# Four projection buffers and two small ones in PSUM, other banks for two kinds of transposes, and a priority for the weights' steps

## The chip, the cores and the metric

The kernel runs on one core of a Trainium2 chip. The metric is the device time of one execution in microseconds. The kernel before takes 2092.26 us, the median of three runs (2090.07 to 2092.64).

The engines are TensorE (PE, matmuls and transposes), VectorE (DVE), ScalarE (ACT), GpSimd (POOL) and SyncE (SP, which issues the DMAs). Each runs its own instructions in order and waits for the others by semaphores. PE writes into PSUM, a memory of eight banks of 128 partitions x 2 KiB; 128x512 values in float32 fill one bank.

## The reference, cut to what matters

One decoder block with two branches from one normalized input, for 2048 tokens and width 1024:

```python
h = rmsnorm(x, norm_g)
glu_in, conv_gate, q, k, v, attn_gate, merge_logits = split(h @ w_in)   # 2048, 1024, 1024, 256, 256, 1024, 2048 columns

a, b = split(glu_in)                       # convolution branch
c = a * sigmoid(b)
c = depthwise_causal_conv(c, 31 taps) + bias
c = silu(layernorm(c))
y_conv = (c * silu(conv_gate)) @ w_conv_out

q, k = rope(q), rope(k)                    # attention branch: 16 query heads, 4 key/value heads of 64
p = softmax(q k^T / 8 over the last 128 keys, with one sink per head)
y_attn = ((p v) * silu(attn_gate)) @ w_attn_out

g_conv, g_attn = split(sigmoid(merge_logits))
x = x + (g_conv * y_conv + g_attn * y_attn) @ w_out
out = rmsnorm(x, final_norm_g)
```

All values are float32. The result has the shape (1, 2048, 1024).

## The kernel before, in words

The tokens are worked in two sweeps of 1024. In each, columns of `w_in` are taken in pieces of 128: h, transposed, lies in SBUF as `hT`, and a piece gives 128 columns of the projection for 1024 tokens, in two halves of 512. To keep float32's accuracy, each number is split in a high and a low part (`whi`, `wlo`; both have type fp32r), and a product is three matmuls: high by high, high by low, low by high. A half is 8 slices of the inner dimension by 3 = 24 matmuls of 128x512 into one PSUM buffer `mm_...` (line 281), and is then read (evacuated) by ACT or DVE.

`load_w` (line 244 on) brings one piece of weights in two halves of the inner dimension: a DMA of the raw values on SP's queue, the cast of the high part on ACT (line 253), and in the first sweep the low part as a difference on POOL (line 242), which is stored in DRAM (`d_lo`, line 263) and only loaded in the second sweep. Buffers for `raw`, `whi` and `wlo` are four each.

PSUM is cut in three pools: `mm` for projections (3 buffers of a bank), `tp` for transposes and value products (3 buffers of a bank), `sc` for attention scores (1 buffer of two banks).

PE's order is written by hand: a generator yields the pieces one after another, and between their matmuls a planner (`Line`) puts the steps of other chains at due times reckoned in a model of PE's pace: the transposes of x (`tpf`, lines 360 and 361), the value transposes (`tpv`, lines 497 and 499), and for each of 32 blocks of attention per sweep the scores (`sc`), the transposes of the probabilities (`tpp`) and the products with the values (`ov`). Instructions on the other engines are ordered by a scheduler: it follows the program's order, and steps inside `tc.high_priority(offset=PRIO)` with PRIO = 60 are taken as if they stood that much earlier. Evacuations and the steps of the chains have it; `load_w` has not, which is called through `prefetch` in `project` one piece ahead.

The values of a sweep are two pieces (`v_item`, i = 0 and 1), each in two halves of 512 tokens. For each of these four, ACT copies the projected half to SBUF (`vs`), PE transposes it in four steps into a `tp` buffer (`tpv`), and ACT and DVE read that buffer: `vf` is ACT's copy of it, `vd` DVE's difference of neighbouring blocks (lines 502 and 503), and `vt` its two parts, high by ACT (line 513) and low by DVE (line 242). Four buffers are asked of a pool of three, whose first is free by the fourth.

The convolution is 31 steps per piece on DVE (`cv`, line 393, 128x1024), 248 per sweep, which the planner lays between other steps. Rope takes the projections of q and k in pairs `a` and `b` (lines 460 to 467, four DVE reads of a pair's buffers per half), joins them on POOL (lines 468 and 469) and splits the result on ACT and DVE. Gates (`ag`, `cg`, `ma`, `mc`) and the sigmoid of the GLU are evacuated by ACT (lines 434 and 415).

Of the kernel before, what the change touches and what calls it, by code (L numbers as in the profile page):

```python
# [12 lines left out]
F32 = mybir.dt.float32  # L13
# [6 lines left out]
P = 128  # L20
# [28 lines left out]
PRIO = 60  # L49
# [4 lines left out]
def hybrid_block(ctx: ExitStack, tc: tile.TileContext, x, par_d, w_in, w_conv, sinks, w_attn, w_out,  # L54
# [5 lines left out]
    slots = ctx.enter_context(tc.tile_pool(name="slots", bufs=1))  # L60
    stage = ctx.enter_context(tc.tile_pool(name="stage", bufs=4))
    work = ctx.enter_context(tc.tile_pool(name="work", bufs=2))
    mm_ps = ctx.enter_context(tc.tile_pool(name="mm_ps", bufs=3, space=bass.MemoryType.PSUM))
    tp_ps = ctx.enter_context(tc.tile_pool(name="tp_ps", bufs=3, space=bass.MemoryType.PSUM))
    sc_ps = ctx.enter_context(tc.tile_pool(name="sc_ps", bufs=1, space=bass.MemoryType.PSUM))
    dram = ctx.enter_context(tc.tile_pool(name="dram", bufs=1, space=bass.MemoryType.DRAM))

# [3 lines left out]
    def f(ap):  # L71
        return ap.bitcast(F32)
# [8 lines left out]
    def slot(tag, shape, dt, name):  # L81
        n = int(np.prod(shape[1:]))
        full = HALO + T + 2 if tag in WIDE else 1024
        t = slots.tile([P, full], dt, tag=tag, name=name)
        v = t[:, 0:n]
        if len(shape) == 3:
            v = v.rearrange("p (a b) -> p a b", b=shape[2])
        elif len(shape) == 4:
            v = v.rearrange("p (a b c) -> p a b c", b=shape[2], c=shape[3])
        return v  # L90

    def t2k(name, dt=F32):
        return work.tile([P, TH], dt, tag="t2k", name=name, bufs=5)
# [140 lines left out]
    line = Line()  # L234
# [6 lines left out]
    def split_lo(out_, full, hi, eng):  # L241
        eng.tensor_tensor(out=out_, in0=full, in1=f(hi), op=ALU.subtract)  # L242

    def load_w(src, name):

        parts = []
        at = lo_at.setdefault((src.tensor.name, src.offset), len(lo_at))
        for kh in range(2):
            raw = stage.tile([P, 4, P], F32, tag="raw", name=f"raw_{name}{kh}")
            nc.sync.dma_start(out=raw, in_=src[:, 4 * kh:4 * kh + 4, :])  # L250
            hi = stage.tile([P, 4, P], F32R, tag="whi", name=f"whi_{name}{kh}")
            lo = stage.tile([P, 4, P], F32R, tag="wlo", name=f"wlo_{name}{kh}")
            act.copy(hi, raw)  # L253
            if (at, kh) in lo_stored:
                nc.sync.dma_start(out=f(lo), in_=d_lo[at, kh])
            else:
                split_lo(lo, raw, hi, pool)
            parts.append((hi, lo))

        def keep(kh):  # L260
            if (at, kh) not in lo_stored:
                lo_stored.add((at, kh))
                nc.sync.dma_start(out=d_lo[at, kh], in_=f(parts[kh][1]))

        return lambda k: (parts[k // 4][0][:, k % 4, :], parts[k // 4][1][:, k % 4, :]), keep

    def project(src, rhs, name, evac, halves=(0, 1)):

        got = {}

        def prefetch():
            got["w"] = load_w(src, name)

        def blocks():
            for half in halves:
                ps = mm_ps.tile([P, TH], F32, tag="mm", name=f"mm_{name}{half}")
                for k in range(KC):
                    whi, wlo = got["w"][0](k)
                    r = rhs(k, half)
                    for i, (a, b) in enumerate(((whi, r[:, 0, :]), (whi, r[:, 1, :]), (wlo, r[:, 0, :]))):  # L280
                        pe.matmul(out=ps, lhsT=a, rhs=b, start=(k == 0 and i == 0),  # L281
                                  stop=(k == KC - 1 and i == 2))
                    if k == KC - 1:
                        with tc.high_priority(offset=PRIO):
                            evac(half, ps)
                    if half == halves[-1] and k % 4 == 3:
                        got["w"][1](k // 4)
                    yield 3 * MM_US

        def by_halves():  # L290
            return [project(src, rhs, f"{name}{h}", evac, (h,)) for h in range(2)]

        return prefetch, blocks, by_halves
# [5 lines left out]
    def make_tiles(tags, half, name):  # L299
        return [slot(tags[half * 8 + k], [P, 2, TH], F32R, f"{name}{half}_{k}") for k in range(KC)]  # L300
# [43 lines left out]
    def build_h_first(half, xs):  # L344

        ss = work.tile([P, 2, 4], F32, tag="ss0", name=f"ssf{half}")
        for j in range(4):
            xt = xs[j]
            sq = slot(C[j], [P, D], F32, f"sqf{half}_{j}")
            act.activation(out=sq, in_=xt, func=AF.Square, accum_out=ss[:, 0, j:j + 1])  # L350
            act.activation(out=ss[:, 1, j:j + 1], in_=ss[:, 0, j:j + 1], func=AF.Sqrt, bias=eps,
                           scale=1.0 / D)
            dve.reciprocal(out=ss[:, 0, j:j + 1], in_=ss[:, 1, j:j + 1])
            dve.tensor_scalar(out=xt, in0=xt, scalar1=ss[:, 0, j:j + 1], scalar2=None, op0=ALU.mult)
        yield 0.0, 6.0
        if half == 1:
            ht[1] = make_tiles(h_tags[0], 1, "hT0_")
        for k in range(KC):
            tp = tp_ps.tile([P, 4, P], F32, tag="tp", name=f"tpf{half}_{k}")
            for j in range(4):  # L360
                pe.transpose(out=tp[:, j, :], in_=xs[j][:, k * P:(k + 1) * P], identity=ident)
            d = ht[half][k].rearrange("p a (j t) -> p a j t", t=P)
            act.activation(out=d[:, 0], in_=tp, func=AF.Copy, scale=g_norm[:, k, :])
            dve.scalar_tensor_tensor(out=d[:, 1], in0=tp, scalar=g_norm[:, k, :], in1=f(d[:, 0]),
                                     op0=ALU.mult, op1=ALU.subtract)
            yield 0.44, 0.8

    def program():
        for s in range(NSWEEP):
            yield from sweep(s)  # L370

    def sweep(s):
# [116 lines left out]
            return store  # L489


        vt, vd = {}, {}

        def v_item(i):
            def chain(half, vs):
                yield 0.0, 7.0
                tp = tp_ps.tile([P, 4, P], F32, tag="tp", name=f"tpv{s}_{i}_{half}")
                for j in range(4):
                    pe.transpose(out=tp[:, j, :], in_=vs[:, j * P:(j + 1) * P], identity=ident)
                vf, d = (t2k(f"{n}{s}_{i}_{half}").rearrange("p (b c) -> p b c", c=P) for n in ("vf", "vd"))  # L500
                act.copy(vf, tp)
                dve.tensor_tensor(out=d[:, 1:4], in0=tp[:, 1:4], in1=vf[:, 0:3], op=ALU.subtract)
                dve.tensor_tensor(out=d[:, 0], in0=tp[:, 0], in1=v_last[:, i], op=ALU.subtract)
                act.copy(v_last[:, i], vf[:, 3])
                for j in range(2):
                    bp = 2 * half + j
                    if i == 0:
                        vt[bp] = slot(AT[bp], [P, 2, NKV, 2 * HD], F32R, f"vt{s}_{bp}")
                        vd[bp] = slot((X + AT[15:])[bp], [P, 2, NKV, 2 * HD], F32R, f"vd{s}_{bp}")
                    for full, to in ((tp, vt), (d, vd)):  # L510
                        part = full[:, 2 * j:2 * j + 2, :].rearrange("p b (g d) -> p b g d", d=HD)
                        hi, lo = (to[bp][:, :, 2 * i:2 * i + 2, a * HD:(a + 1) * HD] for a in range(2))
                        act.copy(hi, part)
                        split_lo(lo, part, hi, dve)
                yield 0.44, 0.0

            def ev(half, ps):
                vs = t2k(f"vs{s}_{i}_{half}")
                act.copy(vs, ps)
                line.start(chain(half, vs))  # L520

            return project(w_in[C_V // P + i], h_rhs, f"v{i}{s}", ev)
# [238 lines left out]
        if s == 0:  # L761
            halves = [item[2]() for item in glu_items(0) + others[:1]]
            halves[0][0][0]()
            xs = load_first(1)
            for _ in build_h_first(0, x_first):
                pass
            line.start(build_h_first(1, xs))
            for half in range(2):
                for i, item in enumerate(halves):
                    yield ((lambda: None) if half == i == 0 else item[half][0],) + item[half][1:]  # L770
            glu_after.pop(0)
# [185 lines left out]
```

## Time and profile before

| | before |
|---|---|
| median of 3 runs | 2092.26 us (2090.07 to 2092.64) |
| profiled execution | 2090.34 us |
| its span, first to last instruction | 2088.4 us |
| PE busy (matmuls) | 2044.0 us, 98% |
| DVE busy | 1391.3 us, 67% |
| ACT busy | 1032.4 us, 49% |
| POOL busy | 483.2 us, 23% |
| mean granted clock of PE | 0.995 |

The profile is that of one execution, whose own time is 1.9 us below the median. "Busy" is the time in which an engine worked on an instruction; a wait is put down to the instruction of another engine that ended last before it. In a row of the timeline stand the start in us, the duration, the engine, the line in the kernel, the operation, output and inputs, shapes, and in brackets the idle time before it and what ended it.

### The profile page before, as it was taken

What the parts mean: (1) busy time and instruction counts of PE and PEld (TensorE: products, weight loads), DVE (VectorE), ACT (ScalarE), POOL (GpSimd) and SP (SyncE); (2) the same over time, 40 slices, a digit from 0 to 9 for tenths busy, and PEclk for the clock granted to TensorE, in tenths of its full rate; (3) what the DMA queues carried; (4) which work ended last, traced back from release to release, by engine and by line L of the source; (5) the groups of instructions that cost most, each with busy time, mean ns of one, the idle gap of its engine ahead of it and who ended that gap; (6) DMA issues with size and microseconds to landing.
All of it is one profiled execution on the core that took longest, in us unless ns stands there. A gap on an engine that the chain in (4) does not pass through costs nothing.

```text
span 2088.4 us, 27452 instructions
## 1 busy us (share of the span) xinstructions
PE 2044.0 (98%) x9256; PEld 1671.7 (80%) x9256; DVE 1391.3 (67%) x1901; ACT 1032.4 (49%) x2265; POOL 483.2 (23%) x336
## 2 busy tenths in 40 slices
PE   7999999998999999999999999999999999999998
PEld 6787888886777888888888888888888888888887
DVE  4979779998988348123559596698888934341324
ACT  6221377666667646112442214766777774621222
POOL 2445433433334222243001131121111110000200
PEclk9999999999999999999999999999999999999999
DMA  7344555554455775646344456555555578574432
GB/s 250 133 144 157 178 166 157 158 163 146 148 152 182 254 238 184 202 142 221 101 151 132 141 161 204 172 158 175 175 163 164 175 225 259 162 236 146 140 119 81
DMA packets 265820, 355.90 MB, mean 170 GB/s; under 512 B 28112, under 2 KB 126544, under 8 KB 265680
## 3 DMA queue, kind: packets, MB, share of 16 engines
q1 hardware_dynamic: 265680, 354.16, 53.3%
q8 instruction: 73, 1.20, 0.2%
q14 instruction: 67, 0.55, 0.1%
HBM read 234.51 MB, written 119.54 MB: 170 GB/s over the span
## 4 chain that ended last, share of the span: by engine, by line
PE 70%; DVE 4%; issue 2%; ACT 1%; DMA 0%; POOL 0%; SPq 0%; DVEq 0%; POOLq 0%; ACTq 0%
PE o L877 9%; PE mm_mc L281 8%; PE mm_yc L281 8%; PE mm_ya L281 8%; PE mm_ma L281 7%; PE mm_ga L281 5%; PE mm_cg L281 5%; PE mm_ag L281 4%; PE mm_gb L281 4%; DVE cv L393 2%; PE mm_q_a L281 2%; PE mm_q_b L281 2%; PE ov L614 2%; PE sc L566 2%; PE mm_v L281 1%
## 5 line engine op out<-in xcount | busy, mean ns | idle before, releaser
L393 DVE SCALAR_TENSOR_TENSOR cv<-glu,par,cv 128x1024 f32<-128x1024 f32 x480 | 675.9, 1408 | 6.7
L605 POOL TENSOR_SCALAR_AFFINE_SELECT pc<-pt 128x1024 fp32r<-128x1024 f32 x60 | 102.7, 1711 | 452.9 <-DVE pt L242 419.6
L877 PE MATMUL o<-wo,mT 128*128 128x512 f32 x768 | 181.3, 394 | 0.0
L877 PEld LDWEIGHTS o<-wo,mT 128*128 128x128 f32 x768 | 143.1, 188 | 32.1
L281 PE MATMUL mm_cg<-hT,whi_cg 128*128 128x512 f32 x512 | 163.2, 400 | 4.6 <-ACT glu L415 3.0
L281 PE MATMUL mm_ma<-hT,whi_ma 128*128 128x512 f32 x512 | 162.9, 399 | 4.0 <-ACT whi_ma L253 4.0
L281 PE MATMUL mm_ga<-hT,whi_ga 128*128 128x512 f32 x512 | 161.0, 395 | 0.2 <-ACT whi_ga L253 0.2
L281 PE MATMUL mm_ag<-hT,whi_ag 128*128 128x512 f32 x512 | 160.9, 395 | 0.0
L281 PE MATMUL mm_gb<-hT,whi_gb 128*128 128x512 f32 x512 | 160.6, 395 | 0.0
L281 PE MATMUL mm_mc<-hT,whi_mc 128*128 128x512 f32 x512 | 159.6, 393 | 0.0
L281 PE MATMUL mm_yc<-uT,whi_yc 128*128 128x512 f32 x512 | 159.4, 392 | 0.0
L281 PE MATMUL mm_ya<-aT,whi_ya 128*128 128x512 f32 x512 | 158.7, 391 | 0.0
L281 PEld LDWEIGHTS mm_cg<-hT,whi_cg 128*128 128x128 f32 x512 | 95.3, 191 | 25.2 <-ACT glu L415 3.4
L281 PEld LDWEIGHTS mm_ma<-hT,whi_ma 128*128 128x128 f32 x512 | 95.1, 190 | 23.9 <-ACT whi_ma L253 4.4
L281 PEld LDWEIGHTS mm_yc<-uT,whi_yc 128*128 128x128 f32 x512 | 96.2, 188 | 21.9
L281 PEld LDWEIGHTS mm_mc<-hT,whi_mc 128*128 128x128 f32 x512 | 96.0, 188 | 21.8
L281 PEld LDWEIGHTS mm_ya<-aT,whi_ya 128*128 128x128 f32 x512 | 96.1, 188 | 20.9
L281 PEld LDWEIGHTS mm_ga<-hT,whi_ga 128*128 128x128 f32 x512 | 94.5, 188 | 20.8 <-ACT whi_ga L253 1.0
L281 PEld LDWEIGHTS mm_gb<-hT,whi_gb 128*128 128x128 f32 x512 | 94.7, 188 | 20.0
L281 PEld LDWEIGHTS mm_ag<-hT,whi_ag 128*128 128x128 f32 x512 | 94.2, 188 | 19.7 <-ACT whi_ag L253 0.3
L584 ACT ACTIVATE ss<-ss,st 128x128 f32<-128x128 f32 x256 | 99.9, 391 | 19.2 <-DVE st L579 18.6
L815 POOL TENSOR_TENSOR lmc<-lmc,mp 128x512 f32<-128x512 f32 x32 | 41.9, 1309 | 275.5 <-DVE lmc L814 267.1
(363 smaller groups left out, 4356.4 us busy)
## 6 DMA issues: line engine op xcount, KB each, us to landing
qk<-d_q SPq DMA_DIRECT2D x256, 64.0 KB, 2.7
d_a<-ss SPq DMA_DIRECT2D x128, 128.0 KB, 1.9
aT<-d_a SPq DMA_DIRECT2D x32, 512.0 KB, 6.1
qk<-d_k SPq DMA_DIRECT2D x240, 64.0 KB, 2.1
raw_gb<-in_w_in_dram SPq DMA_DIRECT2D x34, 256.0 KB, 4.0
raw_ga<-in_w_in_dram SPq DMA_DIRECT2D x34, 256.0 KB, 3.4
raw_ag<-in_w_in_dram SPq DMA_DIRECT2D x32, 256.0 KB, 3.8
d_ag<-ag SPq DMA_DIRECT2D x32, 256.0 KB, 2.1
```

Of the source, the lines that this page charges most:

```text
L281: pe.matmul(out=ps, lhsT=a, rhs=b, start=(k == 0 and i == 0), stop=(k == KC - 1 and i == 2))
L393: dve.scalar_tensor_tensor(out=cv[c], in0=glu[c][:, j:j + T], scalar=tap(c, j), in1=cv[c], op0=ALU.mult, op1=ALU.add)
L566: pe.matmul(out=o, lhsT=q[:, h, :], rhs=r, start=(j == 0), stop=(j == 1))
L584: act.activation(out=sb[:, h, :], in_=sb[:, h, :], func=AF.Exp, scale=SCALE, bias=ngm[:, h:h + 1], accum_out=den[:, h:h + 1])
L605: pool.affine_select(out=pc, in_=f(pt), pattern=[[0, 2], [0, GQ], [1, P]], compare_op=ALU.is_ge, fill=0.0, base=0, channel_multiplier=-1)
L614: pe.matmul(out=ov, lhsT=vv, rhs=pp[:, i % 2], start=(i == 0), stop=(i == nm - 1))
L815: pool.tensor_tensor(out=g, in0=g, in1=mp[e][:, half * TH:(half + 1) * TH], op=ALU.add)
L877: pe.matmul(out=ps, lhsT=a[:, c0:c0 + P], rhs=r, start=(k == 0 and i == 0), stop=(k == KC - 1 and i == 2))
```

## The change

Four edits:

- The pool of projection buffers has 4 banks and the pool of small buffers 2.
- The first transposes of x (`tpf0`, half 0) take their buffers from the projection pool, those of half 1 from the small pool as before.
- The value transposes of the two halves of a piece share one tile of two banks in the pool of the scores, each half in a bank of its own; before, each had a tile of the small pool.
- The loads of the weights and their casts and splits are emitted with a priority: offset PRIO when the planner's time is past 30, else the same wrapper with offset 0.

```diff
-    mm_ps = ctx.enter_context(tc.tile_pool(name="mm_ps", bufs=3, space=bass.MemoryType.PSUM))
-    tp_ps = ctx.enter_context(tc.tile_pool(name="tp_ps", bufs=3, space=bass.MemoryType.PSUM))
+    mm_ps = ctx.enter_context(tc.tile_pool(name="mm_ps", bufs=4, space=bass.MemoryType.PSUM))
+    tp_ps = ctx.enter_context(tc.tile_pool(name="tp_ps", bufs=2, space=bass.MemoryType.PSUM))
     sc_ps = ctx.enter_context(tc.tile_pool(name="sc_ps", bufs=1, space=bass.MemoryType.PSUM))
@@ project
         def prefetch():
-            got["w"] = load_w(src, name)
+            with tc.high_priority(offset=PRIO if line.t > 30.0 else 0):
+                got["w"] = load_w(src, name)
@@ build_h_first
         for k in range(KC):
-            tp = tp_ps.tile([P, 4, P], F32, tag="tp", name=f"tpf{half}_{k}")
+            pool_, tag = ((mm_ps, "mm"), (tp_ps, "tp"))[half]
+            tp = pool_.tile([P, 4, P], F32, tag=tag, name=f"tpf{half}_{k}")
@@ v_item
-        vt, vd = {}, {}
+        vt, vd, tpv = {}, {}, {}
 
         def v_item(i):
             def chain(half, vs):
                 yield 0.0, 7.0
-                tp = tp_ps.tile([P, 4, P], F32, tag="tp", name=f"tpv{s}_{i}_{half}")
+                if half == 0:
+                    tpv[i] = sc_ps.tile([P, 2, 4, P], F32, tag="sc", name=f"tpv{s}_{i}")
+                tp = tpv[i][:, half]
                 for j in range(4):
                     pe.transpose(out=tp[:, j, :], in_=vs[:, j * P:(j + 1) * P], identity=ident)
```

PE's instructions stand in the same order in both kernels. What they wait for differs. On PE, the place of the second and third group of value transposes in the first sweep (`tpv` with `vs_0_1` and `vs_1_0`; `mm_v` is the projection of v, `mm_q_a` the first of q), before:

```order
L281 MATMUL mm_v_792<-hT_1_0_313,wlo_v_660 128x512
L499 MATMUL tpv_0_1_796<-ident_r,vs_0_1_725 128x128 [waits Activation_49]
L281 MATMUL mm_v_792<-hT_1_1_314,whi_v_659 128x512 x2
...
L281 MATMUL mm_q_a_858<-hT_0_0_124,wlo_q_a_731 128x512 [waits Pool_49]
L499 MATMUL tpv_1_0_862<-ident_r,vs_1_0_790 128x128 [waits Activation_49]
L281 MATMUL mm_q_a_858<-hT_0_1_125,whi_q_a_730 128x512 x2
```

and in the changed kernel:

```order
L282 MATMUL mm_v_792<-hT_1_0_313,wlo_v_660 128x512
L503 MATMUL tpv_0_748<-ident_r,vs_0_1_725 128x128 [waits DVE_49]
L282 MATMUL mm_v_792<-hT_1_1_314,whi_v_659 128x512 x2
...
L282 MATMUL mm_q_a_857<-hT_0_0_124,wlo_q_a_731 128x512 [waits Pool_49]
L503 MATMUL tpv_1_861<-ident_r,vs_1_0_790 128x128 [waits DVE_49]
L282 MATMUL mm_q_a_857<-hT_0_1_125,whi_q_a_730 128x512 x2
```

The second group writes the tile of the first (`tpv_0_748`), and both wait for a count of DVE's semaphore where they waited for one of ACT's.

On ACT, at the start (`hT_0` are the scaled transposes of x's first half, `sqf` the squares of its second half, `whi_gb_000` and `whi_gb_001` the two halves of the first weight), before:

```order
L253 CAST whi_gb_000_139<-raw_gb_000_137 128x512
L253 CAST whi_gb_001_145<-raw_gb_001_143 128x512
L363 ACTIVATE hT_0_4_128<-tpf_4_206,par 128x512
L363 ACTIVATE hT_0_5_129<-tpf_5_213,par 128x512
L350 ACTIVATE sqf_0_235,ssf_234<-xf_0_149 128x1024
L363 ACTIVATE hT_0_6_130<-tpf_6_220,par 128x512
```

and in the changed kernel:

```order
L253 CAST whi_gb_000_139<-raw_gb_000_137 128x512
L365 ACTIVATE hT_0_4_128<-tpf_4_206,par 128x512
...
L351 ACTIVATE sqf_1_240,ssf_234<-xf_1_151 128x1024
L365 ACTIVATE hT_0_7_131<-tpf_7_227,par 128x512
L352 ACTIVATE ssf_234<-ssf_234,eps_t 128x1
L351 ACTIVATE sqf_2_245,ssf_234<-xf_2_153 128x1024
L253 CAST whi_gb_001_145<-raw_gb_001_143 128x512
```

The cast of the second half now stands behind three of the four squares; on SP's queue its load stands behind the first three loads of that half of x, where it stood ahead of them.

On ACT, near the end of the first sweep's attention (block 2_7's exponentials and scaled copies `ss`, block 2_6's cast `pt`, the weight `ma_01`), before:

```order
L584 ACTIVATE ss_2_7_5081,st_2_7_5084<-ss_2_7_5081,st_2_7_5084 128x128
L599 CAST pt_2_6_5161<-tpp_2_6_5155 128x512
L589 ACTIVATE ss_2_7_5081<-ss_2_7_5081,st_2_7_5084 128x128 x4
L253 CAST whi_ma_01_5133<-raw_ma_01_5131 128x512
L617 COPY ss_2_5_4801<-ov_2_5_5184 64x256 x2
```

and in the changed kernel:

```order
L588 ACTIVATE ss_2_7_5079,st_2_7_5082<-ss_2_7_5079,st_2_7_5082 128x128
L253 CAST whi_ma_01_5131<-raw_ma_01_5129 128x512
L593 ACTIVATE ss_2_7_5079<-ss_2_7_5079,st_2_7_5082 128x128 x4
L603 CAST pt_2_6_5159<-tpp_2_6_5153 128x512
L621 COPY ss_2_5_4799<-ov_2_5_5182 64x256 x2
```

The weight's cast has moved ahead of the four scaled copies and of the cast of `pt`. Seven second weight halves in the first sweep have moved in this manner.

## The prediction

> **What bounds the kernel now.** I read the page first: which engine is full, and whether the share of the others says anything.
>
> ```profile
> span 2088.4 us, 27452 instructions
> ...
> PE 2044.0 (98%) x9256; PEld 1671.7 (80%) x9256; DVE 1391.3 (67%) x1901; ACT 1032.4 (49%) x2265; POOL 483.2 (23%) x336
> ```
>
> TensorE (PE) is short of the span by 44 us. All that buffers and priorities can win lies in those 44 us and in matmuls that run at a lower clock; all that they can lose is new idle time on PE. So next, PE's busy time by stretches (columns: stretch, its length, busy time and count on each engine, granted clock, DMA share, GB/s):
>
> ```profile
> 310.00:360.00 50.00, 48.68 (x231) 39.79 (x231) 48.42 (x64) 34.21 (x76) 19.09 (x13) 1.00 0.52 158
> ...
> 460.00:510.00 50.00, 45.92 (x215) 36.48 (x214) 49.35 (x60) 36.57 (x78) 14.60 (x9) 1.00 0.49 151
> 510.00:560.00 50.00, 45.08 (x198) 36.44 (x198) 43.20 (x58) 30.40 (x76) 19.39 (x13) 0.93 0.46 141
> 560.00:610.00 50.00, 46.74 (x218) 37.51 (x217) 41.59 (x56) 36.37 (x87) 19.35 (x13) 1.00 0.52 153
> 610.00:660.00 50.00, 45.90 (x206) 37.08 (x205) 49.49 (x62) 33.51 (x75) 15.78 (x10) 0.93 0.52 163
> 660.00:1130.00 470.00, 470.00 (x2098) 384.39 (x2097) 225.97 (x375) 192.68 (x422) 110.94 (x83) 1.00 0.56 184
> ...
> 1160.00:1500.00 340.00, 340.00 (x1571) 280.26 (x1570) 269.44 (x349) 181.17 (x415) 60.50 (x38) 1.00 0.57 172
> ```
>
> From 660 us on PE is never idle. The second sweep (from about 1100) has nothing to win, and whatever PE loses there, or still has to its debit at 660, arrives at the end in full. Before 660 the attention stage (235 to 660) holds 17.7 us of idle PE in five of these stretches (1.32 + 4.08 + 4.92 + 3.26 + 4.10), and VectorE (DVE) is the fullest of the others there. What PE waits for, over the whole span (total, times, longest):
>
> ```profile
> PE mm_ma L281 <- ACT whi_ma L253: 4.0, 1, 4.0
> PE mm_q_b L281 <- DVE rb_q__1_1524 L467: 3.4, 1, 3.4
> PE mm_cg L281 <- ACT glu L415: 3.0, 1, 3.0
> ...
> PE tpv L499 <- ACT vs L519: 2.1, 1, 2.1
> ...
> PE mm_q_b L281 <- DVE ra_q__0_1408 L461: 1.3, 1, 1.3
> ...
> PE tpf L361 <- DVE hT L364: 0.5, 1, 0.5
> ```
>
> The `mm_q_b` waits and the `mm_cg` wait are for a projection buffer to be emptied; `mm_ma` waits for a weight's cast. These are what the fourth buffer and the priority reach. But DVE and ScalarE (ACT) have waits of their own between 235 and 700 us:
>
> ```profile
> DVE pt L242 <- ACT pt L599: 24.5, 8, 3.8
> ...
> DVE glu L419 <- PE mm_ga L281: 4.9, 1, 4.9
> ```
> ```profile
> ACT ss L621 <- DVE ss L619: 50.4, 28, 3.3
> ```
>
> Their big waits are for each other; the one on PE is at the stage's start, 4.9 us. So in that stage softmax, value products and convolution run as a chain on DVE and ACT with a pace of its own, and PE's idle time is mostly PE keeping step with it.
>
> **The value transposes.** This is the largest term. Rows of PE, DVE and ACT around the first sweep's, then PE and DVE in the second:
>
> ```profile
> 85.63 0.60 PE L499 MATMUL tpv<-ident_r,vs 128*128 128x128 f32 x4
> ...
> 93.93 0.66 PE L499 MATMUL tpv<-ident_r,vs 128*128 128x128 f32 x4 [2.11 <-ACT vs L519]
> ```
> ```profile
> 79.36 12.35 DVE L393 SCALAR_TENSOR_TENSOR cv<-glu,par,cv 128x1024 f32<-128x1024 f32 x8
> ...
> 95.68 0.42 DVE L242 TENSOR_TENSOR vt<-tpv,vt 128x256 fp32r<-128x256 f32 x1
> 96.02 0.55 DVE L502 TENSOR_TENSOR vd<-tpv,vf 128x384 f32<-128x384 f32 x1
> ...
> 98.88 0.41 DVE L242 TENSOR_TENSOR vt<-tpv,vt 128x256 fp32r<-128x256 f32 x1
> ...
> 106.21 0.41 DVE L242 TENSOR_TENSOR vt<-tpv,vt 128x256 fp32r<-128x256 f32 x1
> ```
> ```profile
> 94.20 0.59 ACT L501 COPY vf<-tpv 128x512 f32<-128x512 f32 x1
> ```
> ```profile
> 1135.84 0.60 PE L499 MATMUL tpv<-ident_r,vs 128*128 128x128 f32 x4
> ...
> 1141.81 0.60 PE L499 MATMUL tpv<-ident_r,vs 128*128 128x128 f32 x4
> ```
> ```profile
> 1139.50 0.42 DVE L242 TENSOR_TENSOR vt<-tpv,vt 128x256 fp32r<-128x256 f32 x1
> ```
>
> The row at 85.63 is the second of four groups (item 0, half 1); it has a buffer of its own and waits for ACT alone. In the changed order it writes the second bank of the tile whose first bank is item 0's half 0, and its wait is one on DVE; so is that of the third group, which takes the tile anew. I read the second's wait as that for DVE's last read of half 0. DVE is late with it: eight convolution steps of 12.35 us stand ahead of the reads, and the last ends at 95.68 + 0.42 = 96.10. PE is in order: its q projection stands behind the transposes. Loss 96.10 - 85.63 = 10.5 us.
>
> Such a gap also costs clock. After the 3.43 us gap of the wait on `rb_q` the trace has
>
> ```profile
> 198.65 1.03 PE L281 MATMUL mm_q_b<-hT,whi_q_b 128*128 128x512 f32 x2 [3.43 <-DVE rb_q__1_1524 L467]
> ...
> 202.37 0.63 PE L281 MATMUL mm_q_b<-hT,whi_q_b 128*128 128x512 f32 x2
> ...
> 204.42 0.62 PE L281 MATMUL mm_q_b<-hT,whi_q_b 128*128 128x512 f32 x2
> ```
>
> nine matmuls in 3.72 us, then nine in 2.05: 1.6 us lost. I add 1.6 for each gap over 3 us. The Trainium skill ("TensorE: Matmul & The Clock Gate", Part 1) says that an idle window of about 3.4 us halves the array's clock and that about 3.4 us of work bring it back; an estimate from that page is 1.7 us a gap, and this row agrees with it, within 0.1 us.
>
> The third group's old wait (2.1) is overtaken by the delay. Its new one: DVE may start on half 1 when ACT's copy (0.59) after the second transposes is done, near 97.5 where it did at 96.02, so the read that begins at 98.88 ends near 101; the group comes at 93.93 - 2.1 + 10.5 = 102.3, or later by the clock. No wait. The fourth must wait for the read that ends at 106.62, moved by 2 to about 108.6, and comes 6 us behind the third, at 108.3 to 110: a few tenths at most. Sum: 10.5 + 1.6 - 2.1 = **+10.0**; bounds +8.4 (no clock lost) and +14 (third and fourth wait 2 us each).
>
> It isn't given back by DVE: that engine waits for PE again at the stage's start, the 4.9 us above, so the delay reaches the attention stage on both.
>
> Second sweep: 1139.50 + 0.42 - 1135.84 = 4.1 us, and 1.6 of clock. The third group comes at 1141.81 + 4.1, and DVE has read half 1 about a microsecond before. PE has no idle time afterwards to take it back: **+5.7**, bounds +4.1 and +7.7.
>
> **The fourth projection buffer** before 235 us. The two `mm_q_b` waits shown, 4.7 us, and 1.6 of clock can go: 6.3. What is late next is a weight's low part behind rope work on GpSimd (POOL), which follows DVE and not PE:
>
> ```profile
> 219.09 1.30 POOL L242 TENSOR_TENSOR wlo_ga<-raw_ga,whi_ga 128x512 fp32r<-128x512 f32 x1 [1.30 <-issue]
> ```
> ```profile
> 223.68 0.39 PE L281 MATMUL mm_ga<-hT,wlo_ga 128*128 128x512 f32 x1
> ```
>
> It ends at 220.39, 3.3 us ahead of its use. PE cannot come earlier by more: **-3.3**, bounds 0 and -6.3.
>
> **Start-up.** The wrapper takes part in the first loads too, with offset 0, and in the new order the second half of the first weight stands behind three loads of x on SP's queue, and its cast on ACT behind the third square of x.
>
> ```profile
> 21.35 0.61 PE L281 MATMUL mm_gb<-hT,whi_gb 128*128 128x512 f32 x2
> ...
> 25.87 0.50 PE L281 MATMUL mm_ga<-hT,wlo_ga 128*128 128x512 f32 x1 [0.70 <-POOL wlo_ga L242]
> ```
> ```profile
> 22.28 0.20 ACT L350 ACTIVATION_READ_ACCUMULATOR sqf<-xf 128x1 f32 x1
> ...
> 23.78 0.62 ACT L253 CAST whi_ga<-raw_ga 128x512 fp32r<-128x512 f32 x1
> ```
>
> That square ends at 22.48, or 22.0 without the cast ahead of it; the cast (0.62, by its neighbour's row) then ends near 22.6. PE needs it at 21.35, or 20.8 if a fourth buffer for `tpf` saves the 0.5 of the last row of PE's waits above: 1.8 us, and the POOL split (1.30) adds 0.85 for the next low part. Gone are the 0.5, and the waits up to 25.87, about 1.2 with what precedes the 0.70. Net 2.65 - 0.5 - 1.2, about **+0.9**; bounds 0 and +2.
>
> **Attention stage, 235 to 660.** The priority puts the casts of second weight halves ahead of the softmax's four exponentials or copies and of the cast of `pt`; the stalls on weights go, and the fourth buffer takes those on evacuation. The most this can bring is the 17.7 us and the clock in the two stretches at 0.93 (0.07 of 50 us each, 7.0): 24.7. But then PE only runs up to the chain. With two `tp` buffers a product `ov` needs the one before it read:
>
> ```profile
> 647.45 0.43 DVE L618 TENSOR_TENSOR ss<-ov,ss 64x256 f32<-64x256 f32 x1
> ```
> ```profile
> 652.54 0.62 PE L614 MATMUL ov<-pt,vt 128*128 128x512 f32 x2
> ```
>
> Freed at 647.88, used at 652.54: PE has 4.7 us of room at the end of the stage, where the idle time stops. **-4.5**. The other bound is +4: seven moved casts at 0.62 us each ahead of `pt`, the thing DVE already waits 24.5 us for, with no gain.
>
> **Sum**: 0.9 + 10.0 - 3.3 - 4.5 + 5.7 = +8.8 us. The profiled execution took 2090.34 us (span 2088.4), 1.9 below the median of the runs. On the execution it makes 2099.1, on the median 2092.26 + 8.8 = **2101**.
>
> **Rivals.**
> *PE takes back the whole stage.* If the chain was late because of PE's stalls and not the reverse, all 24.7 go, and the 6.3 too: 0.9 + 10.0 - 6.3 - 24.7 + 5.7 = -14.4, 2078. For it: DVE is idle 8.4 us in 560 to 610. Against: DVE at 49.49 of 50 in 610 to 660, and no wait of it on PE. Chance 0.15.
> *Half of it*: the chain speeds up a little, 12 to 13 us come back: 2092 to 2094. Chance 0.13.
> *The new waits on DVE name reads long done*, so the value transposes cost nothing and their old 2.1 goes: 0.9 - 2.1 - 3.3 - 4.5 = -9, 2083. The Trainium skill ("PSUM — Partial Sum Buffer", on bank collisions) says that engines on different banks run clean; by that the two halves need no wait on each other, and only the program's own semaphore could hold PE. Against: the order has the wait on DVE in place of that on ACT at the second group. Chance 0.07.
> *The chain itself gets slower*: casts ahead of `pt`, and `tpp` and `ov` held by two buffers. From the point where the room of 4.7 us is used up, each microsecond on DVE's side is one on PE's: no gain in the stage, +4 there, and +4 for the third and fourth transposes: 8.8 + 4.5 + 4 + 4 = +21, 2113. Chance 0.15.
> The forecast has 0.50, with a range of its own of 2095 to 2108.
>
> **Numbers.** 0.2% of 2092 us, 4.2 us, is what a measurement tells from no change. Faster takes the first and third rival, less a little at the edge: 0.20. Same takes the half case and the lower edge of the forecast: 0.15. Slower 0.65. A range from 2080 to 2112 leaves out the far ends of the first and of the last rival.
>
> **What would show it.** After the change, PE's waits should name DVE `vt` ahead of a `tpv` with some 10 us in the first sweep and 4 in the second, each followed by matmuls at 0.4 us; the `mm_q_b` waits should shrink, `whi_ma` go; PE in 235 to 660 should wait on `sc`, `tpp` or `ov` instead. The prediction is wrong if `tpv` waits for ACT or not at all, or if PE's idle time in 460 to 660 falls by 15 us or more with no new waits.

## The result, and the profile after

The changed kernel is slower: 2107.52 us (median of 6 runs, 2105.11 to 2110.66) against 2091.36 us before (6 runs, 2090.07 to 2092.64). The ratio is 1.0079, with a 95% interval of 1.0069 to 1.0089, that is +16.2 us. The profiled execution took 2109.34 us (span 2107.5), 19.0 us more than that of before; it lies 1.8 us above its median, that of before 1.0 below.

PE's waits in the changed kernel (total, times, longest):

```profile
PE tpv L503 <- DVE vt L242: 14.0, 2, 10.4
PE tpp L598 <- DVE pt L242: 12.4, 10, 2.1
...
PE ov L618 <- DVE ss L622: 5.5, 4, 2.3
...
PE mm_gb L282 <- DVE ra_q__0_1577 L463: 1.7, 1, 1.7
PE mm_gb L282 <- ACT whi_gb L253: 1.7, 1, 1.7
PE mm_ma L282 <- ACT whi_ma L253: 1.6, 1, 1.6
```

The value transposes `tpv` wait for DVE in both sweeps, 10.4 and 3.6 us. The long waits of before on `rb_q`, on the GLU's evacuation and on `whi_ma` are gone or shorter. In their place stand ten waits on `tpp` and four on `ov`, 17.9 us together: the small buffers. Stretches of the changed kernel, same columns as in the prediction, and behind them the one of before from 1130 to 1160:

```profile
85.00:110.00 25.00, 14.64 (x59) 11.75 (x58) 22.92 (x29) 7.58 (x20) 4.60 (x3) 0.80 0.24 70
...
410.00:460.00 50.00, 46.96 (x224) 38.39 (x223) 48.99 (x62) 32.13 (x76) 18.92 (x12) 1.00 0.50 155
610.00:660.00 50.00, 45.27 (x205) 36.33 (x204) 43.50 (x59) 34.83 (x82) 14.63 (x10) 0.97 0.48 148
660.00:1130.00 470.00, 469.81 (x2103) 384.18 (x2102) 228.76 (x386) 199.19 (x442) 111.96 (x85) 1.00 0.56 183
1130.00:1160.00 30.00, 26.37 (x108) 21.20 (x107) 28.04 (x33) 9.98 (x22) 3.78 (x3) 0.89 0.46 154
1160.00:1500.00 340.00, 340.00 (x1564) 279.96 (x1563) 264.94 (x349) 176.35 (x403) 58.16 (x38) 1.00 0.55 167
```
```profile
1130.00:1160.00 30.00, 30.00 (x139) 24.51 (x139) 28.91 (x45) 11.59 (x31) 1.50 (x3) 1.00 0.32 100
```

The holes are at 85 to 110 and at 1130 to 1160 (before, PE had no idle time in the second), and the clock falls to 0.80 and 0.89 there. In the attention stage PE's idle time has not become less, it is only spread more evenly: in the seven stretches of 50 us from 310 to 660 it is 21.7 us in all, where it was 18.3.

Since PE's instructions stand in the same order in both kernels, the time at which the same instruction starts in the two traces gives the loss as it grows (us):

```
PE instruction                        before    after     later by
first sweep, k projection              34.91     37.24      2.33
q projection, before its first wait   175.09    187.76     12.68
first scores (stage starts)           235.00    244.63      9.62
ov near the stage's end               652.54    664.97     12.42
value projection, second sweep       1130.05   1142.88     12.83
q projection after it                1160.04   1179.20     19.16
```

So the parts are: start-up +2.3, first value transposes +10.4, fourth projection buffer -3.1, attention stage +2.8, second value transposes +6.3 (and +0.4 between). The rows of the two large parts, on PE and DVE:

```profile
98.48 1.11 PE L503 MATMUL tpv<-ident_r,vs 128*128 128x128 f32 x4 [10.36 <-DVE vt L242]
99.25 1.20 PE L282 MATMUL mm_v<-hT,whi_v 128*128 128x512 f32 x2
...
1152.45 1.11 PE L503 MATMUL tpv<-ident_r,vs 128*128 128x128 f32 x4 [3.63 <-DVE vt L242]
```
```profile
81.70 12.34 DVE L395 SCALAR_TENSOR_TENSOR cv<-glu,par,cv 128x1024 f32<-128x1024 f32 x8
...
98.01 0.41 DVE L242 TENSOR_TENSOR vt<-tpv,vt 128x256 fp32r<-128x256 f32 x1
```

The second group starts at 98.48, 0.06 us after DVE's last read of the first half ends at 98.42, as the shared tile demands. The third and fourth groups do not wait.

And the attention stage: DVE's reads of two `ov` and a later `ov` on PE in the changed kernel, and the first of these reads before:

```profile
661.91 0.41 DVE L622 TENSOR_TENSOR ss<-ov,ss 64x256 f32<-64x256 f32 x1
...
664.05 0.43 DVE L622 TENSOR_TENSOR ss<-ov,ss 64x256 f32<-64x256 f32 x1
```
```profile
664.97 0.62 PE L618 MATMUL ov<-pt,vt 128*128 128x512 f32 x2
```
```profile
645.31 0.41 DVE L618 TENSOR_TENSOR ss<-ov,ss 64x256 f32<-64x256 f32 x1
```

DVE is 16.6 us later there, where it was 9.6 later at the stage's start: the chain on DVE and ACT lost 7.0 us within the stage. PE, 652.54 - 645.31 = 7.2 us behind that read before, is 3.1 behind it now: it caught up 4.2 us, and lost the rest with the chain. In the prediction's own measure, from the end of the next read (664.05 + 0.43) to that `ov`, 0.5 us of room are left of 4.7.

### The profile page after: what moved, and what is told of

Same layout as the page of the kernel before. It is cut to its first block, busy times and chain, and to the rows that moved or that the text cites. A ratio compares the mean times of both kernels' runs of the same rounds, so it can differ in the third digit from the quotient of the medians.

```text
span 2107.5 us, 27428 instructions
## 1 busy us (share of the span) xinstructions
PE 2048.4 (97%) x9256; PEld 1675.4 (79%) x9256; DVE 1392.9 (66%) x1901; ACT 1032.4 (49%) x2265; POOL 477.3 (23%) x336
```

## The experiments

All times are medians, with 95% intervals of the ratio to the kernel before. Its median was 2091.6 us in the first two groups of four runs, 2090.5 in the next three and 2090.6 in the last. "The chain" below is the first row `ss<-ov` of DVE above (661.91 in the changed kernel), against 645.31 before, less what PE's first scores of the stage are late.

### 1. The changed kernel with a buffer for each half of the value transposes

```diff
-                if half == 0:
-                    tpv[i] = sc_ps.tile([P, 2, 4, P], F32, tag="sc", name=f"tpv{s}_{i}")
-                tp = tpv[i][:, half]
+                tp = tp_ps.tile([P, 4, P], F32, tag="tp", name=f"tpv{s}_{i}_{half}")
```

> The changed kernel, but each half of the value transposes has a buffer of its own in the small pool again; four projection buffers, two small ones and the priority stay. Theory A (the changed kernel loses 10.4 us in the first sweep and 6.3 in the second because the transposes of a half wait for DVE's last read of the other half's bank of the same tile): both PE waits of tpv on DVE vt disappear, and the time falls by 13 to 17 us, from 2107.5 to 2091 to 2094; with two small buffers the third group may still wait up to 2 us in the first sweep. Rival B (the wait is only where PE is held anyway, and the attention stage's own pace sets the end): 2104 or more.

Measured: 2094.72 us, 12.8 less than the changed kernel (ratio to before 1.0021, 1.0012 to 1.0030). PE's waits:

```profile
PE tpp L596 <- DVE pt L242: 12.2, 8, 2.1
...
PE ov L616 <- DVE ss L620: 5.5, 5, 2.3
PE tpv L501 <- DVE vt L242: 4.3, 1, 4.3
```

In the second sweep nothing is left of it, and in the first the third group waits 4.3 us, since two small buffers stand where three stood. At the q projection (175.09 before) this kernel is 3.8 us later, the changed one 12.7. The rival is out. The saving, 12.8, is a shade under the 13 expected, since the third group's wait was put at up to 2 and is 4.3.

### 2. The shared tile alone

The kernel before with the edit of `v_item` only.

> The kernel before with one edit: the value transposes of a piece share a tile of two banks in the pool of the scores. Theory A: PE waits 10.4 us for DVE vt in the first sweep and 3.6 in the second, with lower clock after each; all of it stays: +14 to +17 us, 2105 to 2108, nearly the whole loss of the change. Rival B: the attention stage takes the first sweep's delay back and only the second sweep's 6 us are left: 2096 to 2099.

Measured: 2106.48 us (ratio 1.0073, 1.0061 to 1.0086), 14.9 us more than before, 92% of the whole loss.

```profile
PE tpv L501 <- DVE vt L242: 14.3, 2, 10.4
```

The same PE instructions are later by 10.12 us at 175.09 of before, 10.10 at 235.00, 10.17 at 652.54 and 15.91 after the second sweep's value transposes. The attention stage gave back nothing: DVE waits for PE at its start and both move by the same amount. The rival (the stage takes the delay back) is out.

### 3. The priority alone

```diff
-            got["w"] = load_w(src, name)
+            if line.t > 30.0:
+                with tc.high_priority(offset=PRIO):
+                    got["w"] = load_w(src, name)
+            else:
+                got["w"] = load_w(src, name)
```

> The kernel before with one edit: the weights' steps have priority once the planner's time is past 30, without any wrapper before that. Theory C (the DVE and ACT chain of the attention stage sets the pace, and casts moved ahead of softmax steps make it slower): the waits on whi and wlo go, waits on sc, tpp or ov come, and the chain is later by 2 to 8 us at 660: the time is between -4 and +3 us of before, 2087 to 2094. Rival D (PE's stalls on weights were the loss): -10 to -15 us, 2076 to 2081.

Measured: 2093.68 us, +2.1 (ratio 1.0011, 1.0002 to 1.0020). The chain is 5.9 us late within the stage, and PE, 0.2 late at its start, is 1.1 late at the `ov` of 652.54 of before: it comes nearer the chain by about 5, but that is moving away. Theory C stands, rival D is out. After 660, where PE was never idle before, it now is, and it is 3.5 us late at 1130.

What delays the chain is seen first on ACT, near 265 us. Before:

```profile
264.37 0.58 ACT L599 CAST pt<-tpp 128x512 fp32r<-128x512 f32 x1
265.24 1.29 ACT L589 ACTIVATE ss<-ss,st 128x128 f32<-128x128 f32 x4 [0.29 <-DVE st L587]
266.43 0.60 ACT L253 CAST whi_ag<-raw_ag 128x512 fp32r<-128x512 f32 x1
```

With the priority alone:

```profile
264.54 0.61 ACT L253 CAST whi_ag<-raw_ag 128x512 fp32r<-128x512 f32 x1
265.41 1.28 ACT L593 ACTIVATE ss<-ss,st 128x128 f32<-128x128 f32 x4 [0.26 <-DVE st L591]
266.60 0.56 ACT L603 CAST pt<-tpp 128x512 fp32r<-128x512 f32 x1
```

The weight's cast takes the place of the cast of `pt`. The four scaled copies are ready a moment later and go ahead of `pt` too, so that `pt` is 2.2 us later (266.60 for 264.37) and not 0.6. In ACT's order one more weight's cast stands ahead of `pt` in 12 blocks of the first sweep's attention, and four more softmax instructions in 6 of them. The section on the change and the prediction counted seven moved casts and not twelve, and the prediction nothing of what passes `pt` along with them. Block by block, `pt` is 2.2 us later than before in the first, 4.7 in the ninth, no later than that in the seven after it, ahead of which no cast has moved, and 6.1 near the end of the stage: it loses where casts have moved.

### 4. Four projection buffers and two small ones alone

> The kernel before with one edit: four projection buffers and two small ones. Theory C: the waits of the q projection on DVE go (-3 to -6 us by 235), in the attention stage tpp and ov wait for DVE's reads of the two small buffers instead of for evacuations: between -4 and +4 us, 2087 to 2095. Rival E (two small buffers are what slows the attention stage by 7 us): +4 to +8 us, 2095 to 2099.

Measured: 2093.34 us, +1.8 (ratio 1.0013, 1.0004 to 1.0022). The chain is 0.3 us earlier within the stage: two small buffers do not slow it, and rival E is out. The trace shows what they cost elsewhere: 3.9 us at the start, all but 0.5 of them where the first transposes of x have two buffers (in the changed kernel they take theirs from the projection pool, so that this cost does not arise), and a wait of 4.4 us of the third value transposes. The q projection gains 7.4 us between 175 and 209 us of before, and 4.3 of it go again by 235.

### 5 and 6. The priority with ACT's cast of `pt` kept ahead, and that cast alone

```diff
-            act.copy(pt[:, 0], tpp)
+            with tc.high_priority(offset=PRIO):
+                act.copy(pt[:, 0], tpp)
```

Run 5 has this and the edit of run 3, run 6 this alone.

> The kernel before with the weights' priority past 30 (as in the run with the priority alone, +2.1 us), and in addition ACT's cast of pt with priority, so that it stands ahead of the moved casts and of the four scaled copies again. Theory C1 (the priority makes the DVE and ACT chain of the attention stage 6 us later because the cast of pt falls behind a weight's cast in twelve blocks and behind four scaled copies in six): the chain is at most 2 us later at 660 than before, PE gains up to the 4.7 us of room, and the time is 2086 to 2090. Rival C2 (the chain is late for another reason, such as casts on ACT at any place or POOL's splits): the chain stays 5 to 6 us late, 2092 to 2095.

> The kernel before with ACT's cast of pt alone raised, no priority for weights: the control of the run with both. Theory C1: PE's stalls on weights stay, the chain is as before or up to 3 us earlier since DVE waits 24.5 us for that cast in all: 2088 to 2092. If it falls below 2086, the cast of pt and not the weights' steps is what a tuned order should move.

Measured: 2090.96 us with both (ratio 0.9997, 0.9988 to 1.0006) and 2094.87 with the cast of `pt` alone (1.0016, 1.0007 to 1.0025). Run 5's time is 0.96 above the range named and its chain 4.3 us late where at most 2 was expected. Run 6 missed as well: 2088 to 2092 was expected, with a chain no later than before. Raising `pt` puts it ahead of other softmax steps than before, and this alone makes the chain 3.1 us late and the kernel 3.2 us slower. Against that control the priority costs the chain 1.2 us instead of 5.9, and makes the kernel 3.9 us faster instead of 2.1 slower. If the two effects add up, which no run shows, the place of `pt` in ACT's order is most of the chain's loss; moving it forward by a priority of its own is no cure.

### 7. A fourth to sixth buffer only where the q projection needs them

```diff
-                ps = mm_ps.tile([P, TH], F32, tag="mm", name=f"mm_{name}{half}")
+                if name[:2] in ("q1", "q2", "q3") and half == 1:
+                    ps = tp_ps.tile([P, TH], F32, tag="tp", name=f"mm_{name}{half}")
+                else:
+                    ps = mm_ps.tile([P, TH], F32, tag="mm", name=f"mm_{name}{half}")
```

> The kernel before, but half 1 of the projections q1 to q3 takes its bank from the small pool, which is idle in that stage: six buffers there, and three and three everywhere else. It tests the term of the fourth buffer by itself. Theory: the waits of mm_q_b on DVE go (5.2 us and 1.6 of clock), POOL's split of a weight's low part is late next, and 3 us are left at 235, kept to the end: 2087.5 to 2089.5. Rival: the attention stage's chain does not move with PE and nothing is left: 2091 to 2092.

Measured: 2090.40 us (ratio 0.9994, 0.9985 to 1.0003): not told from no change, and between the two ranges named. PE gains 7.4 us between 175 and 209 us, as with four buffers, and then meets one wait for a weight's cast, followed by matmuls at the low clock:

```profile
221.02 1.22 PE L284 MATMUL mm_ga<-hT,whi_ga 128*128 128x512 f32 x2 [3.08 <-ACT whi_ga L253]
...
223.04 1.05 PE L284 MATMUL mm_ga<-hT,whi_ga 128*128 128x512 f32 x2
```

In the changed kernel the same lateness is met in three waits of 1.7 us and less, without low clock, and 3.1 us are left of the 7.4; here it is 0.8.

### 8. The changed kernel with three and three buffers

> The changed kernel with three projection buffers and three small ones as before; the shared tile, the first transposes in the projection pool and the priority stay. Theory (PE's 18 us of waits on tpp and ov with two small buffers are only the place where PE keeps step with the chain, which the priority makes late): the waits move to sc and to evacuations, the chain stays 6 to 8 us late, the q projection's 3 us come back as a loss: 2107 to 2111. Rival (two small buffers cost time of their own in the attention stage): 2100 to 2105.

Measured: 2109.01 us (ratio 1.0083, 1.0069 to 1.0097). PE no longer waits for `tpp` on DVE; its waits go back to evacuations, `sc` and the q projection. The chain is 6.1 us late within the stage, against 7.0 with two small buffers. The waits on small buffers in the changed kernel were the place where PE kept step, and at most 1 us of the cause.

### 9 to 12. Towards a kernel that is faster than both

> The kernel before with priority for one weight alone: ma0_0, whose cast PE waits 4.0 us for near 630 with some 2.5 us of lower clock after it. In ACT's order one cast of pt falls behind. Theory (at the stage's end PE has 4.7 us of room against the chain, and stalls before it count only as far as that room): nearly all that the priority can bring comes from this one place: the chain at most 1.5 us later, PE 3 to 5 us earlier after 660, time 2087 to 2089. Rival: another stall takes its place at once (sc or tpp near 640) and nothing is left, 2091 to 2092.

> As the run before, and every fourth projection buffer of q1 to q3 comes from the small pool, so that four buffers rotate there and three and three stand everywhere else. The changed kernel gained 3.1 us from four buffers by 235, in three short gaps; borrowing every second one gained 0.8 (one gap of 3.1 us with lower clock after it). Theory: 3 us more than the run with ma0_0 alone, 2084 to 2086. Rival: the gap comes back and it is 2086.5 to 2088.5.

> As the run before, and the planner asks for the value transposes 10 us after their half's copy instead of 7, so that the third group comes some 3 us later on PE and doesn't wait 2.1 to 2.2 us for ACT's copy (with 1 to 1.6 us of lower clock in some executions). Theory: DVE waits for PE at 139 us, so the gain is kept: 2 to 4 us less than the run before, 2080 to 2084. Rival: DVE's reads fall behind further convolution steps and the fourth group or the q projection waits for them: no gain, 2084 to 2087.

Measured: 2090.85 us (ratio 1.0004, 0.9995 to 1.0012), 2089.06 (0.9992, 0.9983 to 1.0001) and 2090.47 (1.0000, 0.9991 to 1.0008). All three lie outside the theory's range and outside the rival's. The first was aimed at the wrong weight, as its PE row shows:

```profile
631.43 1.22 PE L286 MATMUL mm_ma<-hT,whi_ma 128*128 128x512 f32 x2 [4.67 <-ACT whi_ma L253]
```

The wait is still there. By the order of the casts it is for the second half of `ma0_2`, not of `ma0_0`. In the second, four buffers rotate in q1 to q3 (every fourth buffer from the small pool), and the stage starts 2.7 us earlier, measured from the lead that PE has after the start-up. In the third the later value transposes lose their wait on ACT's copy, but the q projection behind them waits for DVE (1.2 us) and a GLU piece for ACT (2.0 us, with lower clock after it), and PE loses 5.3 us between 110 and 175: its rival has the mechanism, though not the time.

The last run has the four rotating buffers and gives the priority to `ma0_2` alone:

```diff
+            early = {"ma0_2": PRIO}.get(name)
+            if early:
+                with tc.high_priority(offset=early):
+                    got["w"] = load_w(src, name)
+            else:
+                got["w"] = load_w(src, name)
```

> The last two runs moved the cast of ma0_0, and their traces still have the wait near 630 (4.0 to 4.7 us): the cast that PE waits for there belongs to the second half of ma0_2. This run has the buffers of the rot4 run, the value transposes' times as before, and priority for ma0_2 alone; in ACT's order that one cast moves ahead of two exponentials and of one cast of pt, by about 5 us. Theory (PE has 4.7 us of room against the chain at the end of the stage): the wait near 630 and its lower clock go, the chain is at most 1 us later, and PE after 660 is 3 to 4.7 us earlier than in the rot4 run: 2084.5 to 2086.5. Rival (the room is used up by waits on sc, tpp or ov close by): 2088 to 2090.

Measured: 2086.56 us, 4.1 less than before (ratio 0.9980, 0.9971 to 0.9989), faster than both kernels and at the upper edge of the range. One cast has moved, and the wait near 630 is gone, so it was for `ma0_2`. The chain is 0.2 us later within the stage, and PE's stretch at its end is nearly full at full clock (45.90 and 0.93 before):

```profile
610.00:660.00 50.00, 49.30 (x231) 40.03 (x230) 49.53 (x63) 33.52 (x75) 17.56 (x10) 1.00 0.52 167
```

PE is 5.8 us ahead of before at the `ov` of 652.54, of which 4.9 were won in the stage. Part of it goes again: PE is 2.6 ahead at 1130, after new waits on ACT's evacuations at 670, 738 and 778 us. The rotating buffers were not run alone, so their share of the 4.1 is not measured.

## Why the prediction was right or wrong

The sign and the cause were right, and the size was half: +8.8 us were forecast, +16.2 measured, inside the forecast's own range of 2095 to 2108 by 0.5 us. The two profiled executions lie 19.0 us apart, and the steps are read from them:

- **Value transposes, first sweep**: forecast +10.0 (10.5 of wait, 1.6 of clock, 2.1 saved), measured +10.4 (10.36 of wait; the rest is clock less the old wait). The order of DVE, the reads and their ends were as said; the third and fourth group come late enough. Runs 1 and 2 show it by removal and by itself.
- **Value transposes, second sweep**: forecast +5.7, measured +6.3: 3.6 of wait and 2.7 of lower clock where 1.6 was put. In runs 2 and 8, with the same tile, PE loses 5.7 and 5.5 us there, 1.8 of each to lower clock, so the 2.7 is one execution's. The estimate of 1.7 from the Trainium skill ("TensorE: Matmul & The Clock Gate", Part 1) is 1.0 too low in the changed kernel's execution and 0.1 in these two; the measurement decides.
- **Fourth buffer before 235**: forecast -3.3, measured -3.1, and for nearly the reason given: what PE gains beyond that it waits for at a weight behind rope's work. The prediction read POOL's split of the low part; run 7 and the changed kernel wait first for the high part's cast on ACT, behind rope's casts there (3.08 and 1.13 us), and for POOL 0.20 and 0.68.
- **Start-up**: forecast +0.9 (bounds 0 and +2), measured +2.3 in this execution. The waits for `whi_gb` and its low part are 1.69 and 0.62 us, as priced; some 1.3 us of lower clock after them were not. With the same start-up edits PE is 0.0 us late at the same place in run 1, where the clock held and x came 0.7 us sooner, and 0.9 in run 8. So this part is between 0 and 2.3, and differs from one execution to the next. That the load and the cast move, the orders show (in run 1 the cast stands behind three squares, in run 3, without a wrapper before 30, where it was). That it is the wrapper which moves them is argued: no run has it without the new place of the first transposes. Its time was not measured apart.
- **Attention stage**: forecast -4.5, measured +2.8. This is the step that failed. Its first half held: PE gains only its room against the chain (4.7 forecast, 4.2 measured). Its second half took the chain's own time as given. The chain lost 7.0 us, and run 3 puts 5.9 of it on the priority. The prediction had a bound for this (seven casts at 0.62 us, +4) and a rival with the mechanism, but no row was read for what happens to `pt` when a cast takes its place.

Of the rivals, "the chain itself gets slower" was the nearest in the stage (+4 there, measured +2.8); its other half, waits of the third and fourth group, did not come. "PE takes back the whole stage" is out by runs 3 and 12: even with its worst stall removed, PE won 4.9 us in the stage. "Half of it" is out because the chain got slower and not faster. "The new waits name reads long done" is out by the 10.36 us. Whether the banks themselves would have allowed it, as the Trainium skill ("PSUM — Partial Sum Buffer", on bank collisions) has it, no run here shows, since the program's own wait held PE.

The chain loses 5.9 and 6.1 us in runs 3 and 8, which have the priority and three small buffers, and 7.0 and 7.1 in the changed kernel and run 1, which have it and two. Without the priority two small buffers cost the chain nothing (run 4). Why they cost some 1 us with it is not explained.

## What to carry to other kernels

In this kernel two halves of one PSUM tile were one buffer to the scheduler, though each had its own bank: the second half's writer may wait for the last reader of the first, and that reader may stand behind long work on its engine, so read the reader's queue before tiles are merged. Where two engines pace a stage between them, a third that waits there wins only its room against that chain (here 4 to 5 us of 18 us idle), and a priority that moves other work into the chain's queue can cost the chain more than it wins (5.9 us for all weights in run 3, 0.2 for one in run 12). Move the one instruction that the last wait names, after its place in the order has been checked against the trace, and not a whole class of them.

## What the runs showed of the hardware

The granted clock after a gap is not a fixed price. Rows of the changed kernel after the 3.63 us gap of the second sweep:

```profile
1153.21 1.20 PE L282 MATMUL mm_v<-hT,whi_v 128*128 128x512 f32 x2
...
1157.20 0.91 PE L282 MATMUL mm_v<-hT,whi_v 128*128 128x512 f32 x2
...
1158.19 0.63 PE L282 MATMUL mm_v<-hT,whi_v 128*128 128x512 f32 x2
```

The matmuls are slow for some 5 us from 1152.45 on and the loss is 2.7 us, where 1.6 was lost in the rows that the prediction used and 1.8 after gaps of 3.96 and 3.65 us at this place in runs 2 and 8. Short gaps differ from execution to execution, too. The wait of the value transposes for ACT's copy, 2.1 us before and 2.2 us in the last run, at the same place (stretch of before, then of the last run):

```profile
85.00:110.00 25.00, 22.89 (x107) 18.53 (x106) 24.79 (x36) 8.64 (x24) 3.91 (x2) 1.00 0.20 66
```
```profile
85.00:110.00 25.00, 22.80 (x100) 18.48 (x99) 24.79 (x36) 8.46 (x23) 3.90 (x2) 0.93 0.22 70
```

With nearly the same idle time the one keeps full clock and the other 0.93, which costs it 1.6 us. Nor does every longer gap cost clock. In run 3 PE runs on at full clock after 3.50 us:

```profile
600.29 0.74 PE L285 MATMUL mm_ma<-hT,whi_ma 128*128 128x512 f32 x2 [3.50 <-ACT glu L419]
...
602.46 0.61 PE L285 MATMUL mm_ma<-hT,whi_ma 128*128 128x512 f32 x2
```

After the start-up, the sixteen gaps of 3.6 us and more in these fourteen traces were all followed by the low clock; of those between 1.6 and 3.5 some were and some were not.
